# Reordering VectorE's splits and the index products of an extra block in a two-layer mixture-of-experts trunk

## The chip, the cores and the metric

One core of one Trainium2 chip runs the kernel. The metric is the device time of one launch in microseconds, the median of several executions. The engines are TensorE (PE in the profile, its weight loads PEld), VectorE (DVE), ScalarE (ACT), GpSimd (POOL) and SyncE (SP, which only issues transfers).

## The reference

Two layers over 512 tokens of width 1024, in float32. Each layer normalises and modulates the tokens, runs two mixers side by side (a chunked matrix memory and attention over a sliding window), merges them, and adds the result to the stream. After that comes the part that matters here, a mixture of 16 experts:

```
t = h.reshape(b * s, d)                      # 512 x 1024
scores = sigmoid(t @ w_router)               # 512 x 16
...                                          # best group of 4, best 2 experts in it
gates = sum(one_hot(idx) * wts)              # two weights for each token
for e in range(16):
    act = silu(t @ w_gate[e]) * (t @ w_up[e])        # 1024 -> 512, twice
    y = y + gates[:, e:e+1] * (act @ w_down[e])      # 512 -> 1024
```

The kernel computes an expert only for the tokens that chose it. The result has to agree with this float32 computation.

## The kernel before

**Experts.** `moe` runs once in each layer. Each expert gets a block of 128 token rows; the five experts with the fewest tokens, at places 4, 6, 8, 10 and 12 of the order (`SMALL`), get 64. An expert's rows are gathered from DRAM by an indirect transfer (`gather`), transposed on TensorE into `XT` (`turn`), multiplied by the gate and up weights (`gateup`), activated, transposed again (`turn_act`), multiplied by the down weights (`down`), and scattered to the DRAM tensor `y2d`. Experts overlap: the loop at the end of `moe` emits, for each expert e, `gateup(e)` with `turn_act(e - 1)` in its middle, then `turn(e + 1)`, then `down(e - 1)`.

**Splits.** A float32 product of a large expert is made of three products in a faster format. Each weight piece of 128 x 1024 is split into a high part `wh`, copied by ScalarE (L1535, L1587), and a low part `wl`, subtracted by VectorE (L1536, L1588); `mm3` (L116 to L118) then makes the products high by high, high by low and low by high. The tags `wh` and `wl` have three buffers each, so at most three pieces are split ahead. Small experts multiply the raw weights directly (L1465 gate and up, L1487 down), so during their gate and up products the split buffers are not needed. The experts in `DN` (all odd places up to 13) split their down weights as well, in four pieces. `turn` of a large expert also splits `XT`, into `XTh` (ScalarE, L1506) and `XTl` (VectorE, L1507), each in two halves.

**Weights.** SyncE streams the weights in chunks of 1 MB through 14 buffers. `pair_of_chunks` takes the next two chunks in a fixed order and issues the loads that may follow; the chunk that comes 14 later reuses a buffer.

**The further block.** An expert with more than 128 tokens spills into an extra block ("over"). `order_places` lists such blocks. `over_rows` reads the first of them: `overflow_next` (L2018 to L2022) writes its expert and block number, two registers are loaded from there (for SyncE and VectorE), and `pick` works out which tokens belong to it. `pick` is also used for the last expert (15), whose rows are combined by a product rather than by a scatter. It has three parts: VectorE builds a 0/1 matrix `osel` (L1634) and the right-hand sides `orv` (seven short operations, L1636 to L1641); TensorE makes eight products `oslot` of them (L1644); VectorE turns `oslot` into token numbers and weights with six short operations (L1645 to L1651; the further block has a seventh, L1665). Both picks share the tiles `osel`, `orv`, `own`, `osf` and `osl`, so VectorE can't fill `osel` for the further block until the products of the last expert's pick have read it. The results are used in `tail`, which has one branch without a further block and one with it.

**Order.** All of an engine's instructions run in one order, fixed when the kernel is built: a planner takes what its own estimates say is ready, earlier code first. Two tools override it. `tc.issue_after(x)` queues what is traced in its block on x's engine behind x; `queue(a, b)` queues b behind a. Neither makes an instruction wait for data. In the loop, `pick` for expert 15 stands after the body of expert 11, VectorE's part behind the activation product of expert 1, and `over_rows` after the body of expert 12, VectorE's part behind that of expert 2.

Of the kernel before, what the change touches and what calls it, by code (L numbers as in the profile page):

```python
# [41 lines left out]
NE = 16  # L42
# [13 lines left out]
DN = (1, 3, 5, 7, 9, 11, 13)  # L56
# [23 lines left out]
def tile_trunk(ctx, tc, x, c, w_ada, b_ada, w_norm1, w_in, conv_w, conv_b, b_igate, b_fgate, w_mnorm,  # L80
# [1252 lines left out]
    def moe(l, raw2, rt):  # L1333
# [110 lines left out]
        stt = {}  # L1444

        def turn_small(e):
# [4 lines left out]
            A.copy(XT, p)  # L1451
            stt["XT", e] = XT.rearrange("p (a b) -> p a b", a=8)

        def gateup_small(e, mid):

            XT = stt["XT", e]
            p = ps("gu")
            for half in range(2):
                if half and mid is not None:
                    mid()  # L1460
                chs = pair_of_chunks()
                for i in range(4):
                    kb = 4 * half + i
                    for g in range(2):
                        stt["gl"] = T.matmul(p[g * 64:g * 64 + 64], XT[:, kb], chs[g][:, i], start=kb == 0, stop=kb == KB - 1)  # L1465
            a_ = mp.tile([128, DE], F32, name="act")
            A.activation(a_[64:128], p[0:64], AF.Silu)
            stt["mul", e] = V.tensor_mul(a_[0:64], p[64:128], a_[64:128])
            stt["act", e] = a_
# [26 lines left out]
        def turn(e, XT=None):  # L1496
            if e in SMALL:
                return turn_small(e)
            if XT is None:
                XT = [mpx.tile([128, D], F32R, tag="XT", name=n, bufs=2).rearrange("p (a b) -> p a b", a=8) for n in ("XTh", "XTl")]  # L1500
            for q in range(2):
                p = ps("XT")
                for i in range(4):
                    T.transpose(p[:, i * 128:(i + 1) * 128], X[e % 2][:, (4 * q + i) * 128:(4 * q + i + 1) * 128], ident)  # L1504
                h_ = XT[0][:, 4 * q:4 * q + 4].rearrange("p a b -> p (a b)")
                A.copy(h_, p)  # L1506
                V.tensor_sub(XT[1][:, 4 * q:4 * q + 4].rearrange("p a b -> p (a b)"), p, h_)  # L1507
            stt["XT", e] = XT

        def turn_first(splits):  # L1510
# [66 lines left out]
        def down(e):  # L1577
            if e in SMALL:
                return down_small(e)
            aT = stt["aT", e]  # L1580
            wd = pair_of_chunks()
            Y = w4(e)
            pd = [ps("down0"), ps("down1")]
            for fb in range(4):
                if e in DN:
                    wh, wl = hl(2)
                    A.copy(wh.rearrange("p a b -> p (a b)"), wd[fb // 2][:, fb % 2])  # L1587
                    V.tensor_sub(wl.rearrange("p a b -> p (a b)"), wd[fb // 2][:, fb % 2], wh.rearrange("p a b -> p (a b)"))  # L1588
                for q in range(2):
                    if e in DN:  # L1590
                        mm3(pd[q], aT[:, 0, fb], aT[:, 1, fb], wh[:, q], wl[:, q], fb == 0, fb == 3)
                    else:
                        T.matmul(pd[q], aT[:, fb], wd[fb // 2][:, fb % 2, q * 512:(q + 1) * 512], start=fb == 0, stop=fb == 3)  # L1593
            for q in range(2):
                V.tensor_mul(Y[:, q * 512:(q + 1) * 512], pd[q], g2[:, q * 512:(q + 1) * 512])
            c = col(e)
            stt["put"] = G.indirect_dma_start(out=y2d, out_offset=bass.IndirectOffsetOnAxis(ap=slot[:, c:c + 1], axis=0),
                                              in_=Y, in_offset=None, bounds_check=2 * S - 1, oob_is_err=False)
# [29 lines left out]
        otok, ltok = [mp.tile([128, TB], F32, name=n, bufs=1) for n in ("otok", "ltok")]  # L1628
        ow, lw = [mp.tile([128, 1], F32, name=n, bufs=1) for n in ("ow", "lw")]

        def pick(e, places, tok, w):

            es_ = ds(e, 1) if not isinstance(e, int) else slice(e, e + 1)
            V.tensor_tensor(osel, places[:, :, None].to_broadcast([128, 2 * TB, 128]),  # L1634
                            iof[:, None, :].to_broadcast([128, 2 * TB, 128]), op=OP.is_equal)
            V.tensor_copy(orv[:, :, 0:2], rv.rearrange("p k t e c -> p (k t) e c")[:, :, es_, :].rearrange("p t o c -> p t (o c)"))  # L1636
            V.tensor_mul(own, top[:, :, :, es_].rearrange("p k t o -> p (k t o)"), wall.rearrange("p k t -> p (k t)"))
            for i in range(2, 5):
                V.tensor_copy(orv[:, :, i], own)
                if i < 4:  # L1640
                    V.tensor_sub(own, own, orv[:, :, i])  # L1641
            p = ps("oslot")
            for t in range(2 * TB):
                T.matmul(p[:, 0:5], osel[:, t], orv[:, t], start=t == 0, stop=t == 2 * TB - 1)  # L1644
            V.tensor_scalar(osf, p[:, 0:1], 4096.0, None, op0=OP.add)  # L1645
            V.tensor_add(osl[:, 0:1], p[:, 1:2], osf)
            V.tensor_reduce(w, p[:, 2:5], axis=AX.X, op=OP.add)

            V.tensor_single_scalar(osl[:, 1:2], osl[:, 0:1], 511 | 4096 | 8192, op=OP.bitwise_and)
            V.tensor_copy(osf, osl[:, 1:2])  # L1650
            V.tensor_sub(tok, osf.to_broadcast([128, TB]), firsts)  # L1651
# [6 lines left out]
        def over_rows():  # L1658

            overflow_next(posB)  # L1660
            e = nc.values_load(ovi[0:1, 0:1], engines=[ET.SP, ET.DVE], min_val=0, max_val=NE - 1)
            be = nc.values_load(ovi[0:1, 1:2], engines=[ET.DVE], min_val=0, max_val=2)
            V.tensor_copy(opos, posB[:, ds(be, 1), :].rearrange("p o t -> p (o t)"))
            pick(e, opos, otok, ow)
            V.tensor_single_scalar(ogi, osl[:, 0:1], 511, op=OP.bitwise_and)  # L1665
            return e

        def over_gather():
            G.indirect_dma_start(out=X[0], out_offset=None, in_=h2d[l],
# [229 lines left out]
        for e in range(NE):  # L1899
# [15 lines left out]
                down(e)  # L1915
            if e == NE - 5:
                with tc.issue_after(stt["mul", 1].ins):
                    pick(NE - 1, pk.rearrange("p k t -> p (k t)"), ltok, lw)
            if e == NE - 4:
                with tc.issue_after(stt["mul", 2].ins):  # L1920
                    oe = over_rows()
            if e == 1:
                with tc.issue_after(stt["mul", e].ins):
                    order_places()
# [21 lines left out]
        with none.Else():  # L1946
            with tc.If(n0 == 1) as one:
                tail(True)
            with one.Else():
                V.tensor_scalar(ovl, ovl, 1.0, None, op0=OP.add)  # L1950
                with tc.For_i(0, n0, 1):
                    e = over_rows()
                    over_gather()
                    turn(NE, XO)
                    oh, hl_ = over_block([over_chunk(e, i, raw2[0]) for i in range(6)])
                    for t in range(TB):
                        for i in range(2):
                            p = ps("rows")
                            for j in range(2):
                                T.matmul(p, oh[:, t * 128:(t + 1) * 128], hl_[j][:, i], start=j == 0, stop=j == 1)  # L1960
                            V.tensor_add(xt[t, i], xt[t, i], p)
                tail(False)
# [178 lines left out]
```

## Time and profile before

| what | value |
|---|---|
| median of 3 runs | 1427.54 us (1427.28 to 1436.03) |
| the profiled execution, its own time | 1431.1 us |
| its span, first to last instruction | 1429.2 us |
| mean granted TensorE clock | 0.974 |
| busy: PE, DVE, ACT, POOL | 93%, 70%, 47%, 14% |
| bytes moved by DMA | 365.09 MB, mean 255 GB/s |

The page's slices give busy tenths for each fortieth of the span (35.7 us). The experts of the first layer lie at about 428 to 716 us, those of the second at about 1100 to 1429 us. In this execution the first layer ends in the branch without a further block and the second in the branch with one. Times of the rows count from the first instruction; "idle before" names the engine's idle time ahead of an instruction and what ended it.

### The profile page before, as it was taken

To read this page: it belongs to the slowest core of one execution; us is meant where nothing else is said; L and a number is where in the kernel's file an instruction comes from. 1 tells how busy PE (TensorE), PEld (TensorE's weight loads), DVE (VectorE), ACT (ScalarE), POOL (GpSimd) and SP (SyncE) were. 2 spreads that over 40 slices of the span, in tenths; PEclk is the share of its full clock that TensorE was granted. 3 is DMA by queue.
4 is the path that set the end of the run, shared out by engine and by line. 5 is a ranking of instruction groups with operands and counts; after the bars stand their busy time and mean duration, and the time that the engine had idled before them with its cause. 6 is when DMAs were issued, how large, how long until landed. Compare 5 with 4: busy or idle time off the path is not lost.

```text
span 1429.2 us, 18477 instructions
## 1 busy us (share of the span) xinstructions
PE 1336.1 (93%) x6407; PEld 980.0 (69%) x6407; DVE 1005.8 (70%) x1941; ACT 678.4 (47%) x1184; POOL 206.4 (14%) x254
## 2 busy tenths in 40 slices
PE   2999999999989999979989999999998999997994
PEld 2776777778876666647568777777887766664662
DVE  5687756778578756657767666656858866765857
ACT  4254335444236545536356335444424655553652
POOL 7500020010011111210230000001001111211023
PEclk9998999999999999999999999999999999998998
DMA  9565465575868999999744433456566999999891
GB/s 313 204 222 164 131 247 177 182 234 181 301 223 278 361 380 381 378 369 384 263 158 148 147 108 129 155 200 170 200 249 238 314 350 390 378 376 381 324 365 64
DMA packets 166499, 365.09 MB, mean 255 GB/s; under 512 B 10549, under 2 KB 41517, under 8 KB 166136
## 3 DMA queue, kind: packets, MB, share of 16 engines
q1 hardware_dynamic: 152928, 327.71, 65.0%
q0 software_dynamic: 12752, 33.92, 6.9%
q10 hardware_dynamic: 712, 2.14, 0.5%
q8 instruction: 54, 0.88, 0.3%
q14 instruction: 53, 0.43, 0.1%
HBM read 346.27 MB, written 26.78 MB: 261 GB/s over the span
## 4 chain that ended last, share of the span: by engine, by line
PE 78%; DVE 11%; DMA 6%; ACT 2%; issue 2%; another core or an unknown queue 0%; ACTq 0%; POOL 0%; DVEq 0%; SPq 0%; POOLq 0%
PE winT L116 5%; PE winT L117 5%; PE winT L118 5%; PE gu L1465 5%; PE down L1593 3%; PE gate L117 3%; PE gate L116 3%; PE gate L118 3%; PE up L117 3%; PE up L118 3%; PE up L116 3%; DMA raw<-in_w_ada_dram 2%; PE downs L1487 2%; PE out L116 2%; PE out L118 2%; PE out L117 2%
## 5 line engine op out<-in xcount | busy, mean ns | idle before, releaser
L1535 ACT CAST wh<-raw 128x1024 fp32r<-128x1024 f32 x168 | 175.9, 1051 | 117.6 <-PE gate L118 82.3
L1536 DVE TENSOR_TENSOR wl<-raw,wh 128x1024 fp32r<-128x1024 f32 x168 | 201.8, 1221 | 34.1 <-ACT wh L1535 33.2
L116 PE MATMUL winT<-hh,wh 128*128 128x512 f32 x416 | 168.1, 405 | 0.5 <-DVE P L882 0.5
L117 PE MATMUL winT<-hl,wh 128*128 128x512 f32 x416 | 165.5, 398 | 0.0
L118 PE MATMUL winT<-hh,wl 128*128 128x512 f32 x416 | 165.3, 397 | 0.0
L483 ACT CAST wh<-raw 128x1024 fp32r<-128x1024 f32 (+1 forms) x59 | 54.2, 930 | 141.6 <-PE winT L117 86.3
L278 DVE SCALAR_TENSOR_TENSOR acc<-raw,cs,acc 128x1024 f32<-128x1024 f32 x70 | 89.6, 1280 | 32.7 <-DMA raw<-in_w_ada_dram 32.0
L116 PEld LDWEIGHTS winT<-hh,wh 128*128 128x128 f32 x416 | 78.9, 190 | 25.1 <-issue 5.1
L118 PEld LDWEIGHTS winT<-hh,wl 128*128 128x128 f32 x416 | 79.1, 190 | 18.7
L117 PEld LDWEIGHTS winT<-hl,wh 128*128 128x128 f32 x416 | 79.2, 190 | 17.6 <-DVE hl L463 0.3
L484 DVE TENSOR_TENSOR wl<-raw,wh 128x1024 fp32r<-128x1024 f32 (+1 forms) x57 | 60.3, 1067 | 25.6 <-ACT wh L483 25.5
L116 PE MATMUL gate<-wh,XTh 128*128 128x512 f32 x176 | 74.6, 424 | 3.0 <-ACT XTh L1523 2.6
L1465 PE MATMUL gu<-raw,XT 128*64 128x512 f32 x320 | 74.7, 597 | 0.7 <-DMA raw<-in_w_up_e_dram 0.7
L1588 DVE TENSOR_TENSOR wl<-raw,wh 128x1024 fp32r<-128x1024 f32 x56 | 66.5, 1219 | 12.0 <-ACT wh L1587 12.0
L117 PE MATMUL gate<-wl,XTh 128*128 128x512 f32 x176 | 73.1, 415 | 1.2 <-DVE wl L1536 1.2
L1395 POOL DMA_INDIRECT X<-h2d,gidx x30 | 38.5, 1283 | 238.7 <-PE XT L1504 103.1
L116 PE MATMUL up<-wh,XTh 128*128 128x512 f32 x176 | 69.9, 397 | 3.0 <-ACT wh L1535 3.0
L118 PE MATMUL gate<-wh,XTl 128*128 128x512 f32 x176 | 71.7, 407 | 0.5
L117 PE MATMUL up<-wl,XTh 128*128 128x512 f32 x176 | 70.2, 399 | 1.9 <-DVE wl L1536 1.9
L118 PE MATMUL up<-wh,XTl 128*128 128x512 f32 x176 | 69.6, 395 | 0.0
L1587 ACT CAST wh<-raw 128x1024 fp32r<-128x1024 f32 x56 | 57.0, 1048 | 13.9 <-PE down L118 7.9
L329 POOL DMA_DIRECT2D modd<-adarow x8 | 4.2, 531 | 406.4 <-DVE adarow L328 406.4
(530 smaller groups left out, 3044.0 us busy)
## 6 DMA issues: line engine op xcount, KB each, us to landing
raw<-in_w_down_e_dram SPq DMA_DIRECT2D x64, 1024.0 KB, 14.1
raw<-in_w_gate_e_dram SPq DMA_DIRECT2D x62, 1024.0 KB, 14.6
raw<-in_w_up_e_dram SPq DMA_DIRECT2D x62, 1024.0 KB, 14.7
raw<-in_w_ada_dram SPq DMA_DIRECT2D x40, 1024.0 KB, 5.1
raw<-in_w_in_dram SPq DMA_DIRECT2D x30, 1024.0 KB, 5.4
sch<-in_w_ada_dram SPq DMA_DIRECT2D x32, 256.0 KB, 6.5
raw<-in_w_out_dram SPq DMA_DIRECT2D x8, 1024.0 KB, 6.6
yk<-y2d SPq DMA_DIRECT2D x8, 1024.0 KB, 15.8
```

Of the source, the lines that this page charges most:

```text
L116: T.matmul(o, lh, rh, start=start, stop=False)
L117: T.matmul(o, lh, rl, start=False, stop=False)
L118: return T.matmul(o, ll, rh, start=False, stop=stop)
L278: V.scalar_tensor_tensor(self.acc, ch[:, a], cs[:, kb:kb + 1], self.acc, op0=OP.mult, op1=OP.add)
L483: A.copy(wh[:, :, a:b], src)
L484: (G if "first" in st else V).tensor_sub(wl[:, :, a:b], src, wh[:, :, a:b])
L1465: stt["gl"] = T.matmul(p[g * 64:g * 64 + 64], XT[:, kb], chs[g][:, i], start=kb == 0, stop=kb == KB - 1)
L1535: A.copy(wh, src)
L1536: stt["split"] = E.tensor_sub(wl, src, wh)
L1587: A.copy(wh.rearrange("p a b -> p (a b)"), wd[fb // 2][:, fb % 2])
L1588: V.tensor_sub(wl.rearrange("p a b -> p (a b)"), wd[fb // 2][:, fb % 2], wh.rearrange("p a b -> p (a b)"))
L1593: T.matmul(pd[q], aT[:, fb], wd[fb // 2][:, fb % 2, q * 512:(q + 1) * 512], start=fb == 0, stop=fb == 3)
```

## The change

There are two parts. `split_down` is a new function that makes one split of a down piece. In `gateup_small(e)`, behind the gate and up products and ahead of the activation, the two down chunks of expert e - 1 are taken from the stream and the first two of its four pieces are split; `down(e - 1)` then makes only the other two. In `turn(e + 1)` the first of the two subtractions of `XTl` is queued behind the second of these splits on VectorE. The two chunks keep their place in the stream, since nothing else takes a chunk between the old place and the new.

`pick` is cut in two: `pick` keeps VectorE's preparation, and `picked` has the eight products and what reads them. The last expert's `picked` moves from the body of expert 11 to that of expert 12, and `over_rows` follows it, no longer behind expert 2's activation product. The further block's `over_picked` moves to expert 14 and its products are queued behind the last gate and up product of that expert.

```
@@ -1451,6 +1451,13 @@
             A.copy(XT, p)
             stt["XT", e] = XT.rearrange("p (a b) -> p a b", a=8)
 
+        def split_down(e, fb):
+            wh, wl = hl(2)
+            src = stt["wd", e][fb // 2][:, fb % 2]
+            A.copy(wh.rearrange("p a b -> p (a b)"), src)
+            stt["sv"] = V.tensor_sub(wl.rearrange("p a b -> p (a b)"), src, wh.rearrange("p a b -> p (a b)"))
+            return wh, wl
+
         def gateup_small(e, mid):
 
             XT = stt["XT", e]
@@ -1463,6 +1470,10 @@
                     kb = 4 * half + i
                     for g in range(2):
                         stt["gl"] = T.matmul(p[g * 64:g * 64 + 64], XT[:, kb], chs[g][:, i], start=kb == 0, stop=kb == KB - 1)
+            if e - 1 in DN:
+                stt["wd", e - 1] = pair_of_chunks()
+                stt["sd", e - 1] = [split_down(e - 1, fb) for fb in range(2)]
+                stt["early"] = stt["sv"]
             a_ = mp.tile([128, DE], F32, name="act")
             A.activation(a_[64:128], p[0:64], AF.Silu)
             stt["mul", e] = V.tensor_mul(a_[0:64], p[64:128], a_[64:128])
@@ -1504,7 +1515,9 @@
                     T.transpose(p[:, i * 128:(i + 1) * 128], X[e % 2][:, (4 * q + i) * 128:(4 * q + i + 1) * 128], ident)
                 h_ = XT[0][:, 4 * q:4 * q + 4].rearrange("p a b -> p (a b)")
                 A.copy(h_, p)
-                V.tensor_sub(XT[1][:, 4 * q:4 * q + 4].rearrange("p a b -> p (a b)"), p, h_)
+                o = V.tensor_sub(XT[1][:, 4 * q:4 * q + 4].rearrange("p a b -> p (a b)"), p, h_)
+                if "early" in stt:
+                    queue(stt.pop("early"), o)
             stt["XT", e] = XT
 
         def turn_first(splits):
@@ -1578,14 +1591,13 @@
             if e in SMALL:
                 return down_small(e)
             aT = stt["aT", e]
-            wd = pair_of_chunks()
+            wd = stt["wd", e] = stt.get(("wd", e)) or pair_of_chunks()
             Y = w4(e)
             pd = [ps("down0"), ps("down1")]
+            sd = stt.get(("sd", e), [])
             for fb in range(4):
                 if e in DN:
-                    wh, wl = hl(2)
-                    A.copy(wh.rearrange("p a b -> p (a b)"), wd[fb // 2][:, fb % 2])
-                    V.tensor_sub(wl.rearrange("p a b -> p (a b)"), wd[fb // 2][:, fb % 2], wh.rearrange("p a b -> p (a b)"))
+                    wh, wl = sd.pop(0) if sd else split_down(e, fb)
                 for q in range(2):
                     if e in DN:
                         mm3(pd[q], aT[:, 0, fb], aT[:, 1, fb], wh[:, q], wl[:, q], fb == 0, fb == 3)
@@ -1628,7 +1640,7 @@
         otok, ltok = [mp.tile([128, TB], F32, name=n, bufs=1) for n in ("otok", "ltok")]
         ow, lw = [mp.tile([128, 1], F32, name=n, bufs=1) for n in ("ow", "lw")]
 
-        def pick(e, places, tok, w):
+        def pick(e, places):
 
             es_ = ds(e, 1) if not isinstance(e, int) else slice(e, e + 1)
             V.tensor_tensor(osel, places[:, :, None].to_broadcast([128, 2 * TB, 128]),
@@ -1639,6 +1651,9 @@
                 V.tensor_copy(orv[:, :, i], own)
                 if i < 4:
                     V.tensor_sub(own, own, orv[:, :, i])
+
+        def picked(tok, w):
+
             p = ps("oslot")
             for t in range(2 * TB):
                 T.matmul(p[:, 0:5], osel[:, t], orv[:, t], start=t == 0, stop=t == 2 * TB - 1)
@@ -1661,9 +1676,12 @@
             e = nc.values_load(ovi[0:1, 0:1], engines=[ET.SP, ET.DVE], min_val=0, max_val=NE - 1)
             be = nc.values_load(ovi[0:1, 1:2], engines=[ET.DVE], min_val=0, max_val=2)
             V.tensor_copy(opos, posB[:, ds(be, 1), :].rearrange("p o t -> p (o t)"))
-            pick(e, opos, otok, ow)
+            pick(e, opos)
+            return e
+
+        def over_picked():
+            picked(otok, ow)
             V.tensor_single_scalar(ogi, osl[:, 0:1], 511, op=OP.bitwise_and)
-            return e
 
         def over_gather():
             G.indirect_dma_start(out=X[0], out_offset=None, in_=h2d[l],
@@ -1915,10 +1933,13 @@
                 down(e)
             if e == NE - 5:
                 with tc.issue_after(stt["mul", 1].ins):
-                    pick(NE - 1, pk.rearrange("p k t -> p (k t)"), ltok, lw)
+                    pick(NE - 1, pk.rearrange("p k t -> p (k t)"))
             if e == NE - 4:
-                with tc.issue_after(stt["mul", 2].ins):
-                    oe = over_rows()
+                picked(ltok, lw)
+                oe = over_rows()
+            if e == NE - 2:
+                with tc.issue_after(stt["gl"].ins):
+                    over_picked()
             if e == 1:
                 with tc.issue_after(stt["mul", e].ins):
                     order_places()
@@ -1950,6 +1971,7 @@
                 V.tensor_scalar(ovl, ovl, 1.0, None, op0=OP.add)
                 with tc.For_i(0, n0, 1):
                     e = over_rows()
+                    over_picked()
                     over_gather()
                     turn(NE, XO)
                     oh, hl_ = over_block([over_chunk(e, i, raw2[0]) for i in range(6)])
```

## Rows read from the trace of the kernel before

**Rows 1.** The page: busy times, and the chain that ended last by engine.

```profile
PE 1336.1 (93%) x6407; PEld 980.0 (69%) x6407; DVE 1005.8 (70%) x1941; ACT 678.4 (47%) x1184; POOL 206.4 (14%) x254
...
PE 78%; DVE 11%; DMA 6%; ACT 2%; issue 2%; another core or an unknown queue 0%; ACTq 0%; POOL 0%; DVEq 0%; SPq 0%; POOLq 0%
```

**Rows 2.** Waits of TensorE over the whole span: in all, times, longest, in us.

```profile
PE oslot L1644 <- DVE orv L1639: 10.6, 2, 5.3
...
PE down L116 <- ACT wh L1587: 3.5, 2, 1.7
...
PE down L117 <- DVE wl L1588: 1.8, 2, 0.9
...
PE down L1593 <- ACT aT L1574: 3.0, 2, 1.5
```

**Rows 3.** Timeline of TensorE, first layer: start, duration, instruction, count, idle before.

```profile
629.77 0.73 PE L116 MATMUL down<-wh,aT 128*128 128x512 f32 x2 [1.75 <-ACT wh L1587]
...
637.94 0.39 PE L118 MATMUL down<-wh,aT 128*128 128x512 f32 x1
...
643.62 0.35 PE L1644 MATMUL oslot<-orv,osel 128*128 128x5 bf16 x8 [5.30 <-DVE orv L1639]
...
648.93 0.40 PE L116 MATMUL up<-wh,XTh 128*128 128x512 f32 x1
...
651.82 0.46 PE L1475 MATMUL aT<-ident,act 64*128 64x64 f32 x4
```

**Rows 4.** Stretches of the first layer: length, busy PE, PEld, DVE, ACT, POOL, PEclk, DMA, GB/s.

```profile
643.60:648.70 5.10, 5.08 (x20) 4.01 (x20) 1.69 (x8) 1.04 (x1) 0.00 (x0) 0.50 1.04 394
...
617.00:638.00 21.00, 17.64 (x78) 9.35 (x76) 10.85 (x18) 8.29 (x10) 2.98 (x2) 0.92 1.02 372
...
638.00:662.00 24.00, 18.70 (x86) 13.12 (x84) 17.48 (x30) 11.10 (x14) 1.92 (x2) 0.86 1.04 401
...
662.00:690.00 28.00, 26.49 (x110) 18.44 (x107) 20.07 (x23) 14.92 (x17) 2.95 (x3) 1.00 0.76 280
```

**Rows 5.** Timeline of VectorE, first layer, experts 10 to 13.

```profile
592.98 3.50 DVE L1588 TENSOR_TENSOR wl<-raw,wh 128x1024 fp32r<-128x1024 f32 x3 [0.25 <-ACT wh L1587]
...
619.00 1.22 DVE L1634 TENSOR_TENSOR osel<-opos,iof 128x1024 bf16<-128x1024 f32 x1
...
628.13 0.69 DVE L1507 TENSOR_TENSOR XTl<-XT,XTh 128x512 fp32r<-128x512 f32 x1 [6.79 <-PE gu L1465]
...
630.15 3.49 DVE L1588 TENSOR_TENSOR wl<-raw,wh 128x1024 fp32r<-128x1024 f32 x3
...
638.29 1.22 DVE L1536 TENSOR_TENSOR wl<-raw,wh 128x1024 fp32r<-128x1024 f32 x1
...
640.02 2.35 DVE L1536 TENSOR_TENSOR wl<-raw,wh 128x1024 fp32r<-128x1024 f32 x2
...
642.29 0.17 DVE L1636 COPY orv<-rv 128x16 bf16 x1
...
643.39 0.18 DVE L1639 CAST orv<-own 128x8 bf16<-128x8 f32 x1
```

**Rows 6.** Timeline of ScalarE, first layer, experts 12 and 15.

```profile
628.67 1.99 ACT L1587 CAST wh<-raw 128x1024 fp32r<-128x1024 f32 x2
...
631.31 1.05 ACT L1587 CAST wh<-raw 128x1024 fp32r<-128x1024 f32 x1 [0.64 <-DMA raw<-in_w_down_e_dram]
...
681.17 1.05 ACT L1535 CAST wh<-raw 128x1024 fp32r<-128x1024 f32 x1 [0.30 <-PE down L118]
```

**Rows 7.** Timeline of SyncE: two weight loads of the first layer are issued.

```profile
612.14 3.55 SPq L1381 DMA_DIRECT2D raw<-in_w_down_e_dram  x2
...
654.36 1.25 SPq L1381 DMA_DIRECT2D raw<-in_w_gate_e_dram  x1
```

**Rows 8.** DMA issues, one in each: the loads of rows 7, us from issue to landing.

```profile
raw<-in_w_down_e_dram SPq DMA_DIRECT2D x1, 1024.0 KB, 16.1
...
raw<-in_w_gate_e_dram SPq DMA_DIRECT2D x1, 1024.0 KB, 18.3
```

More of the change, by code (lines that the diff above doesn't have):

```diff
@@ L1452, in turn_small, with split_down @@
             stt["XT", e] = XT.rearrange("p (a b) -> p a b", a=8)
+        def split_down(e, fb):
+            wh, wl = hl(2)
+            src = stt["wd", e][fb // 2][:, fb % 2]
+            A.copy(wh.rearrange("p a b -> p (a b)"), src)
+            stt["sv"] = V.tensor_sub(wl.rearrange("p a b -> p (a b)"), src, wh.rearrange("p a b -> p (a b)"))
+            return wh, wl
         def gateup_small(e, mid):
@@ L1465, in gateup_small @@
                         stt["gl"] = T.matmul(p[g * 64:g * 64 + 64], XT[:, kb], chs[g][:, i], start=kb == 0, stop=kb == KB - 1)
+            if e - 1 in DN:
+                stt["wd", e - 1] = pair_of_chunks()
+                stt["sd", e - 1] = [split_down(e - 1, fb) for fb in range(2)]
+                stt["early"] = stt["sv"]
             a_ = mp.tile([128, DE], F32, name="act")
@@ L1506, in turn @@
                 A.copy(h_, p)
-                V.tensor_sub(XT[1][:, 4 * q:4 * q + 4].rearrange("p a b -> p (a b)"), p, h_)
+                o = V.tensor_sub(XT[1][:, 4 * q:4 * q + 4].rearrange("p a b -> p (a b)"), p, h_)
+                if "early" in stt:
+                    queue(stt.pop("early"), o)
             stt["XT", e] = XT
@@ L1580, in down @@
             aT = stt["aT", e]
-            wd = pair_of_chunks()
+            wd = stt["wd", e] = stt.get(("wd", e)) or pair_of_chunks()
             Y = w4(e)
             pd = [ps("down0"), ps("down1")]
+            sd = stt.get(("sd", e), [])
             for fb in range(4):
                 if e in DN:
-                    wh, wl = hl(2)
-                    A.copy(wh.rearrange("p a b -> p (a b)"), wd[fb // 2][:, fb % 2])
-                    V.tensor_sub(wl.rearrange("p a b -> p (a b)"), wd[fb // 2][:, fb % 2], wh.rearrange("p a b -> p (a b)"))
+                    wh, wl = sd.pop(0) if sd else split_down(e, fb)
                 for q in range(2):
@@ L1629, in moe, with pick @@
         ow, lw = [mp.tile([128, 1], F32, name=n, bufs=1) for n in ("ow", "lw")]
-        def pick(e, places, tok, w):
+        def pick(e, places):
             es_ = ds(e, 1) if not isinstance(e, int) else slice(e, e + 1)
@@ L1641, in pick, with picked @@
                     V.tensor_sub(own, own, orv[:, :, i])
+        def picked(tok, w):
             p = ps("oslot")
@@ L1663, in over_rows, with over_picked @@
             V.tensor_copy(opos, posB[:, ds(be, 1), :].rearrange("p o t -> p (o t)"))
-            pick(e, opos, otok, ow)
+            pick(e, opos)
+            return e
+        def over_picked():
+            picked(otok, ow)
             V.tensor_single_scalar(ogi, osl[:, 0:1], 511, op=OP.bitwise_and)
-            return e
         def over_gather():
@@ L1917, in moe @@
                 with tc.issue_after(stt["mul", 1].ins):
-                    pick(NE - 1, pk.rearrange("p k t -> p (k t)"), ltok, lw)
+                    pick(NE - 1, pk.rearrange("p k t -> p (k t)"))
             if e == NE - 4:
-                with tc.issue_after(stt["mul", 2].ins):
-                    oe = over_rows()
+                picked(ltok, lw)
+                oe = over_rows()
+            if e == NE - 2:
+                with tc.issue_after(stt["gl"].ins):
+                    over_picked()
             if e == 1:
@@ L1952, in moe @@
                     e = over_rows()
+                    over_picked()
                     over_gather()
```

## Prediction

> **What bounds the kernel now.** I read the page first: TensorE is busy 93% of the span and carries 78% of the chain that ended last [rows 1]. So only time in which TensorE stands still, or runs slowly, can be won. Next I listed what TensorE waits for. Its longest wait is the one the change points at: `oslot` on `orv`, twice, 5.3 us each, once in each layer. Beside it stand two short waits of the down products on their splits, 1.7 and 0.9 us in each layer, and one of 1.5 us on `aT` [rows 2].
>
> The timeline shows the place. `down` of expert 11 can start at 629.77, after 1.75 us of idling, and ends at about 638.2 (its last product starts at 637.94 and takes 0.23 of TensorE's time). The next instruction is the first `oslot` of the further block, at 643.62. Twelve gate products follow up to 648.93, in 5.1 us, 0.43 each; the next twelve, up to the transposes at 651.82, take 2.9, some 0.23 each, TensorE's usual pace [rows 3]. There the first half of expert 13 ends. The granted clock over 643.6 to 648.7 is 0.50, the lower of its two levels (1.2 GHz), after the engine had stood still; it is below 1 as well, 0.92 on average, over 617 to 638, where the two short waits lie [rows 4]. VectorE shows why `orv` is late: in its order it stands behind three splits of expert 13, and starts at 642.29 [rows 5].
>
> The second thing to see is the weight stream. The DMA engines are at 1.02 to 1.04 of their time from 617 to 662, at 372 to 401 GB/s, and fall to 0.76 only after that [rows 4]. A faster TensorE meets weights that come no sooner.
>
> **The change part by part.** *(a) The further block's products leave the place behind `down` of expert 11.* Removed there: 5.3 us of standing still, and the low clock after it, 12 products at 0.43 instead of 0.23, 2.3 us. The eight products are moved, not removed. What is late next: the splits of expert 13. VectorE's first `wl` ends at 639.5, the next two at 641.2 and 642.4 [rows 5]. A piece feeds six products, 1.4 us. So without the stop the first piece is done at 639.5 + 5 x 0.23 = 640.7, the second at 642.4, the third at 643.9. The fourth needs a buffer that the first frees (cast 1.05, subtraction 1.22, ready at 643.6), and is done at 645.4. Before, the same four pieces ended at 651.8. Gain: 6.4 us.
>
> Against that stands VectorE's own work for the picks. The last expert's products now come after the body of expert 12, so what depends on them may fall behind `down` of 11 too: six short operations like the one at 643.39 (1.0 us), `osel` (1.22 us, at 619.00 before), `orv` (642.29 to 643.57, 1.3 us) [rows 5]. Pieces go round a ring of three buffers: cast 1.05, subtraction 1.22, products 1.4 and about 0.5 for two hand-overs (the first is 0.3 in [rows 6]) make 4.2 us, and TensorE uses three pieces in 4.2. So VectorE time put into that ring is lost. With all 3.5 us in it the gain is 2.9 us, with none 6.4. I take `orv` where it is now, behind the third split, and the rest beside the transposes and small down products: 5.1 us.
>
> TensorE itself waits for nothing new at the last expert's products: their `orv` is filled long before, their results are wanted in `tail`. The further block's stand behind expert 14's gate and up products, over 20 us after `orv`; 0.4 us of TensorE each, as before. SyncE reads the block's expert number from what VectorE writes; that read stands among the weight loads as before, and a late one would hold them. With 16 to 18 us from issue to landing [rows 8] some 6 MB are on the way, so a hold below 10 us starves nothing. GpSimd gets nothing new.
>
> *(b) Two down splits first on VectorE.* At experts 4, 6, 8 and 10 they already are: at expert 10 three splits run in one piece from 592.98, ahead of activation and `XTl` [rows 5]. Only at expert 12 does VectorE stand at an `XTl` for 6.79 us, until the gate and up products free its buffer at 628.13, with the splits behind it [rows 5]. Only there can the change matter. The stop of 1.75 us is ScalarE's cast, which starts at 628.67 [rows 6]. Its chunk was issued at 612.14 and took 16.1 us: it landed at 628.2, just as the gate and up products ended at 628.0 [rows 3, 7, 8]. So the cast can come 0.4 us earlier at most. VectorE's first `wl` starts at 630.15 although the cast ends at 629.7: another 0.4. But the activation product and both `XTl`, 2.0 us, which ran during the wait for the cast, then fall between the second and the third split. The third piece's chunk, cast at 631.31 after a wait for DMA, sets that split: it ends at about 635.0 instead of 633.6 (630.15 + 3.49). Bounds: 0.5 us lost, 1.0 won; I take 0.3 won, since both ends hang on one late chunk.
>
> Taking the two chunks earlier changes no order among SyncE's loads, and the stream is full.
>
> *Sum.* 5.1 + 0.3 = 5.4 us in each layer. The second layer has the same waits [rows 2], so 10.8 us for both. **The cap.** Expert 15's chunks are the test. Its first lands at 654.36 + 18.3 = 672.7, the next some 2.7 us later (1 MB at 386 GB/s, between 372 and 401), at 675.4. ScalarE casts the third piece from it at 681.17, 5.8 us later, and ahead of the `aT` that TensorE waits for [rows 2, 6 to 8]. So nearly all of 5.4 us fits, and not much more. DMA has (1 - 0.76) x 28 = 6.7 us of room in 662 to 690 [rows 4], so the tail's loads can follow.
>
> How the weights go is where a page bears. The Trainium skill, "HBM Reference", section Specifications (TRN2), gives a core that streams alone about 425 GB/s. Here the full stretches show 372 to 401. By the page's figure a chunk would take an estimated 2.5 us, the stream would gain on TensorE, and the cap would not bind; the sum would then be its upper bound, 14.8 us.
>
> The profiled execution took 1431.1 us, 3.6 above the median. For it the sum gives 1420.3; for the median 1427.5 - 10.8 = **1416.7**.
>
> **The rivals.** *VectorE takes the place of the wait.* All its picking work lies in the ring: 2.9 us a layer, less 0.5: 2.4, so 1422.7. For it: the new code puts the last expert's products behind `down` of 11. Against: in the rows of before, that work filled idle time. Chance 0.22.
>
> *The weights don't bind so early, and nothing of the picking is in the way:* 6.4 + 1.0 = 7.4 a layer, 14.8 in all: 1412.7; with the low clock around the short waits gone too (21 x (1 - 0.92) = 1.7 us a layer [rows 4]) 1409.3. For: the DMA share falls after 662. Against: the cap. Chance 0.14.
>
> *The stream is the bound already:* the time comes back as waits for `raw`, 1 us a layer is left, 1425.5. For: the DMA share of 1.04. Against: the third piece of expert 15 has its chunk 5.8 us before its cast. Chance 0.07. The Trainium skill, "DMA: Bandwidth & Descriptors", section Where 436 GB/s comes from, says that for transfers from HBM the memory side binds at about 358 GB/s; by it the stretch would be bound all through, and the sum some 2 us. The trace is above that figure, at 372 to 401, and does not agree.
>
> *Slower: the clock.* The long stop goes, but short waits for `wl` stay at the start of expert 13. If the clock, low behind 629.7, stays low through its 48 products, that is 48 x 0.2 = 9.6 us, and with some 1.5 us of waits 11.1 against the 5.3 + 2.3 removed: 3.5 us lost a layer, 1434.5. It decides if the granted clock is still 0.5 at 649 us; with expert 14 low as well, another 9.6 a layer, it is 1453.7. Against: after each stop here it was back in about 5 us of unbroken products [rows 3, 4]. Chance 0.05.
>
> *The change does not do what it says:* the old place is filled by the last expert's products. They have their operands, so nothing is lost; this is in the forecast.
>
> **The numbers.** Forecast 0.52, spread over 4.3 to 6.4 us a layer: 1414.7 to 1418.9. The range of 8 in 10 takes in the first rival, and the second down to 1410: 1410 to 1424.5. A measurement of this kernel can't tell less than about 1% from no change, here 14.3 us, 1413.3. Faster by more than that needs the second rival and a little of the forecast: 0.16. Slower by over 1%: the last rival whole, since a clock that stays low would hardly stop at one expert: 0.05. Within 1%: 0.79.
>
> **What would show it.** In the changed trace: no wait of `oslot` on `orv`; eight `oslot` products behind the gate and up products of expert 14; VectorE's order at expert 12 with two L1588 ahead of L1507; the first half of expert 13 ending 5 to 6 us sooner after expert 12's products; a clock of 1.00 there; `aT` of expert 14 no longer waiting, or waiting on a cast that waits for DMA (the cap). I am wrong if TensorE's idle time at experts 12 and 13 shrinks and the time up to the last scatter does not, or if `osel` and `orv` stand between the splits of expert 13 and hold them by over 3 us.

## The result and the profile after

| | median, us | runs | ratio to the kernel before, 95% interval |
|---|---|---|---|
| before | 1429.55 (1423.71 to 1436.03) | 8 | |
| after | 1420.89 (1416.95 to 1425.86) | 8 | 0.9938 (0.9914 to 0.9962) |

The change saves 0.6%, some 8.9 us (5.4 to 12.3). The profiled execution took 1419.82 us, its span is 1418.0.

What TensorE waits for, whole span (us in total, times, longest):

```profile
PE gate L117 <- DVE wl L1549: 5.8, 6, 2.3
PE down L117 <- DVE wl L1458: 5.4, 8, 1.2
PE down L116 <- ACT wh L1457: 3.6, 2, 1.8
```

and one line of the kernel before that belongs beside them:

```profile
PE gate L117 <- DVE wl L1536: 1.2, 4, 0.4
```

The wait of `oslot` on `orv` [rows 2] is gone. The waits on `wl` have grown, on the gate products from 1.2 to 5.8 us, on the down products from 1.8 [rows 2] to 5.4. TensorE's timeline in the first layer shows where they are (start, duration, in brackets the idle time ahead and its releaser):

```profile
629.05 0.73 PE L116 MATMUL down<-wh,aT 128*128 128x512 f32 x2 [1.83 <-ACT wh L1457]
629.63 0.35 PE L1659 MATMUL oslot<-orv,osel 128*128 128x5 bf16 x8
...
634.50 0.50 PE L117 MATMUL down<-wl,aT 128*128 128x512 f32 x1 [1.18 <-DVE wl L1458]
...
636.89 0.40 PE L116 MATMUL gate<-wh,XTh 128*128 128x512 f32 x1
...
649.73 3.65 PE L1498 MATMUL downs<-raw,aT 128*64 128x512 f32 x16
...
656.13 0.50 PE L117 MATMUL gate<-wl,XTh 128*128 128x512 f32 x1 [2.32 <-DVE wl L1549]
```

Expert 15's index products stand inside `down` of expert 11. Expert 13's gate follows that `down` at 636.89 without a gap, 7 us earlier than before [rows 3]. Then, at expert 14, TensorE stands still for 2.32 us. VectorE shows why:

```profile
628.05 0.69 DVE L1479 TENSOR_TENSOR act<-gu,act 64x512 f32<-64x512 f32 x1
629.03 2.36 DVE L1458 TENSOR_TENSOR wl<-raw,wh 128x1024 fp32r<-128x1024 f32 x2 [0.28 <-ACT wh L1457]
631.42 0.69 DVE L1518 TENSOR_TENSOR XTl<-XT,XTh 128x512 fp32r<-128x512 f32 x1
...
632.10 1.22 DVE L1646 TENSOR_TENSOR osel<-opos,iof 128x1024 bf16<-128x1024 f32 x1
633.23 2.35 DVE L1458 TENSOR_TENSOR wl<-raw,wh 128x1024 fp32r<-128x1024 f32 x2
...
653.43 1.39 DVE L1502 TENSOR_TENSOR Y<-downs,g 64x512 f32<-64x512 f32 x2 [1.97 <-PE downs L1498]
654.85 3.50 DVE L1549 TENSOR_TENSOR wl<-raw,wh 128x1024 fp32r<-128x1024 f32 x3
```

Two down splits do stand early at expert 12. `osel` then stands ahead of the third, which makes the 1.18 us above. And the `Y` of expert 12, which needs TensorE's down products, stands ahead of expert 14's first splits, although ScalarE had cast the high parts of the first two by 652.67, 2.2 us before VectorE takes them up:

```profile
650.68 1.99 ACT L1548 CAST wh<-raw 128x1024 fp32r<-128x1024 f32 x2 [0.25 <-DMA raw<-in_w_gate_e_dram]
```

In the kernel before, the two stood the other way round:

```profile
656.89 2.36 DVE L1536 TENSOR_TENSOR wl<-raw,wh 128x1024 fp32r<-128x1024 f32 x2 [0.66 <-ACT wh L1535]
...
662.60 1.39 DVE L1491 TENSOR_TENSOR Y<-downs,g 64x512 f32<-64x512 f32 x2 [0.42 <-PE downs L1487]
```

The granted clock in four stretches of after (length, busy time and pieces of PE, PEld, DVE, ACT, POOL, then clock, DMA share, GB/s): expert 13; the end of the stop at expert 14 in the first layer; what follows it there; what follows the same stop in the second layer.

```profile
637.00:649.70 12.70, 12.70 (x61) 9.88 (x59) 9.74 (x12) 7.61 (x9) 1.80 (x1) 1.00 1.03 396
653.30:656.10 2.80, 0.51 (x3) 0.19 (x1) 2.62 (x4) 1.04 (x1) 1.00 (x1) 1.00 1.04 402
656.10:662.00 5.90, 5.87 (x27) 4.83 (x28) 4.93 (x5) 3.39 (x4) 0.76 (x1) 1.00 1.02 406
1321.30:1327.00 5.70, 5.70 (x20) 4.63 (x21) 3.52 (x4) 1.75 (x3) 0.73 (x1) 0.72 1.03 413
```

Expert 13 runs at full clock, where its first half had 0.50 [rows 4]. Behind the stop at expert 14 the clock stays full in the first layer and is 0.72 in the second.

**One measure for all kernels.** In both profiles, and in those of the experiments, time is counted from the end of expert 10's last down product. Given is how long after it expert 12's down products start, expert 14's up products end, and expert 15's last product ends.

| kernel | layer 1, us | layer 2, us | ratio to before |
|---|---|---|---|
| before | 41.6, 57.0, 93.1 | 40.9, 56.4, 92.9 | |
| before, again | 41.3, 56.8, 92.8 | 40.9, 56.4, 92.8 | 0.9985 (0.9958 to 1.0011) |
| after | 32.2, 51.1, 87.0 | 31.7, 52.1, 88.5 | 0.9938 (0.9914 to 0.9962) |
| after, again | 32.7, 51.6, 87.5 | 31.8, 52.0, 88.4 | 0.9959 (0.9938 to 0.9981) |
| picks only | 31.7, 52.2, 88.1 | 32.4, 51.3, 87.6 | 0.9957 (0.9931 to 0.9982) |
| splits only | 38.6, 54.1, 90.2 | 38.6, 54.1, 90.5 | 0.9998 (0.9973 to 1.0023) |
| order at 14 | 32.0, 48.4, 84.3 | 31.8, 48.1, 84.4 | 0.9893 (0.9856 to 0.9930) |
| order at 14, again | 32.1, 48.4, 84.4 | 31.7, 48.1, 84.4 | 0.9904 (0.9868 to 0.9941) |
| `orv` early | 35.4, 55.7, 91.1 | 34.2, 54.7, 90.5 | 0.9987 (0.9961 to 1.0013) |
| `orv` early, order at 14 | 34.7, 51.0, 86.4 | 34.2, 50.6, 86.4 | 0.9931 (0.9908 to 0.9955) |
| `osel` later | 35.5, 51.9, 87.8 | 35.0, 51.4, 87.7 | 0.9954 (0.9933 to 0.9975) |
| cast first | 32.7, 49.1, 85.0 | 33.6, 49.9, 86.3 | 0.9922 (0.9898 to 0.9945) |
| all early | 30.9, 47.7, 83.3 | 32.1, 48.5, 84.6 | 0.9907 (0.9875 to 0.9938) |
| all early, old place | 31.4, 47.7, 83.1 | 32.1, 48.5, 84.3 | 0.9902 (0.9867 to 0.9937) |

So after gains 9.4 and 9.2 us up to expert 12, gives 3.5 and 4.9 back by the end of expert 14, and keeps 6.1 and 4.4.

### The profile page after: what moved, and what is told of

The parts are those of the page before. It is cut to its first block, busy times and chain, and to the rows that moved or that the text cites. A ratio compares the mean times of both kernels' runs of the same rounds, so it can differ in the third digit from the quotient of the medians.

```text
span 1418.0 us, 18485 instructions
## 1 busy us (share of the span) xinstructions
PE 1328.5 (94%) x6407; PEld 973.3 (69%) x6407; DVE 1005.3 (71%) x1941; ACT 679.1 (48%) x1184; POOL 207.1 (15%) x254
## 4 chain that ended last, share of the span: by engine, by line
PE 43%; DVE 5%; issue 1%; DMA 1%; ACT 1%; another core or an unknown queue 0%; POOL 0%; DVEq 0%; ACTq 0%; SPq 0%; POOLq 0%
PE winT L116 4%; PE winT L117 3%; PE winT L118 3%; PE gu L1472 3%; PE gate L117 2%; PE down L1605 1%; PE up L117 1%; PE gate L118 1%; PE up L118 1%; PE gate L116 1%; PE up L116 1%; PE downs L1498 1%; PE tok L118 1%; PE tok L116 1%; PE out L116 1%; PE out L118 1%
## 5 line engine op out<-in xcount | busy, mean ns | idle before, releaser
L1458 DVE TENSOR_TENSOR wl<-raw,wh 128x1024 fp32r<-128x1024 f32 x56 | 66.8, 1220 | 10.8 <-ACT wh L1457 10.8
```

The costliest lines, as they stand in the source:

```text
L1458: stt["sv"] = V.tensor_sub(wl.rearrange("p a b -> p (a b)"), src, wh.rearrange("p a b -> p (a b)"))
```

## The experiments

**One part alone.** Picks only: the changed kernel without

```
-            if e - 1 in DN:
-                stt["wd", e - 1] = pair_of_chunks()
-                stt["sd", e - 1] = [split_down(e - 1, fb) for fb in range(2)]
-                stt["early"] = stt["sv"]
```

> The changed kernel without its early down splits: only the picking is parted and moved. My theory (the wait of the first index product on orv is the whole change, 5 us a layer and more behind it; the early splits are worth 0.3 us a layer): 0.993 to 0.996 of the kernel before, within 2 us of the changed kernel's 8.9 us gain, no wait oslot<-orv, the product of expert 14's first gate half still waiting some 2 us for wl. The rival (the early splits carry a good part, since VectorE has room only before the last half of XT's rest): half the gain, 0.997 or more, with waits on wl at expert 12 of 2 us and more in each layer.

Splits only: the changed kernel with the picking where it was.

```
                     pick(NE - 1, pk.rearrange("p k t -> p (k t)"))
+                    picked(ltok, lw)
             if e == NE - 4:
-                picked(ltok, lw)
-                oe = over_rows()
-            if e == NE - 2:
-                with tc.issue_after(stt["gl"].ins):
+                with tc.issue_after(stt["mul", 2].ins):
+                    oe = over_rows()
                     over_picked()
```

> The changed kernel with the further block's picking back in its old place: only the early splits are left. My theory: within 0.2% of the kernel before (0.998 to 1.001), the wait oslot<-orv still at 10 us in two pieces, a wait of down(11) on wh of under 2 us a layer. The rival (the splits carry a part of their own): 0.997 or less.

Picks only keeps 5.0 and 5.3 us a layer, as much as the whole change: my theory. Its ratio, 0.9957, lies in the range that I gave. Splits only met its forecast in time (0.9998, and the wait on `orv` stays), but not the theory behind it: the stretch is 2.9 and 2.4 us shorter, where 0.3 was expected. TensorE's timeline of splits only:

```profile
628.13 0.50 PE L117 MATMUL down<-wl,aT 128*128 128x512 f32 x1 [0.53 <-DVE wl L1458]
628.47 0.40 PE L118 MATMUL down<-wh,aT 128*128 128x512 f32 x1
...
639.21 0.35 PE L1659 MATMUL oslot<-orv,osel 128*128 128x5 bf16 x8 [5.53 <-DVE orv L1651]
```

and of the kernel before at the same product:

```profile
631.42 0.62 PE L117 MATMUL down<-wl,aT 128*128 128x512 f32 x1 [0.92 <-DVE wl L1588]
631.84 0.63 PE L118 MATMUL down<-wh,aT 128*128 128x512 f32 x1
```

The wait of 0.92 us became 0.53, and the products behind it run at full pace instead of half. The clock over all of `down` of 11 is 0.80 before and 1.00 here:

```profile
629.80:638.20 8.40, 7.48 (x24) 5.49 (x25) 5.58 (x6) 5.06 (x5) 0.00 (x0) 0.80 1.01 366
```

```profile
626.90:633.60 6.70, 6.17 (x24) 4.32 (x25) 5.61 (x6) 5.06 (x5) 0.00 (x0) 1.00 1.05 382
```

The timed runs of splits only show none of these 5 us; that is taken up below.

**VectorE's order at expert 14.** The changed kernel, and where `gateup(14)` splits its gate chunk:

```
+                        if e == NE - 2 and half == 0 and p is pg and j == 1:
+                            queue(stt["split"], stt["Y", e - 2])
```

`stt["Y", 12]` is expert 12's first `Y` product.

> The changed kernel, and on VectorE expert 14's first two gate splits stand ahead of expert 12's two Y products. Theory (what was given back at expert 14 is VectorE's order alone: two splits whose ScalarE half is long done stand behind a Y that waits for the down products): the wait of expert 14's first gate product falls from 2.3 us to under 0.5 in both layers, the low clock behind it in the second layer goes, and the time is 3 to 8 us under the changed kernel's, 0.988 to 0.992 of the kernel before. Rival (the stream of weights is the next limit): the wait moves to the ScalarE casts and their DMA one or two chunks later, and the time stays within 1.5 us of the changed kernel's, 0.993 to 0.995.

> The changed kernel with expert 14's first two gate splits ahead of expert 12's Y products, once more: 0.987 to 0.992 of the kernel before, the stretch from expert 10's last product to expert 15's last 84.3 us in both layers, if what it gave the first time was the order and not the run.

```profile
652.31 2.36 DVE L1550 TENSOR_TENSOR wl<-raw,wh 128x1024 fp32r<-128x1024 f32 x2
654.59 1.38 DVE L1502 TENSOR_TENSOR Y<-downs,g 64x512 f32<-64x512 f32 x2
```

```profile
654.30:657.10 2.80, 2.80 (x12) 2.28 (x13) 2.75 (x4) 1.63 (x2) 0.85 (x1) 1.00 1.04 391
1323.90:1329.60 5.70, 5.70 (x31) 4.75 (x30) 5.37 (x7) 3.87 (x5) 1.76 (x1) 1.00 1.03 410
```

VectorE's order and two windows of the first of the two runs: TensorE is busy all through where it had stood, and the clock is full. What after gave back is kept, 8.8 and 8.5 us a layer, and 8.7 and 8.5 in the second run. It was VectorE's order, and not the stream, which ran at 391 to 410 GB/s meanwhile.

**The wait without the move.** The kernel before; only the register load is parted, so that the planner is free to place VectorE's early:

```
-            e = nc.values_load(ovi[0:1, 0:1], engines=[ET.SP, ET.DVE], ...)
+            e, ev = [nc.values_load(ovi[0:1, 0:1], engines=[g], ...) for g in (ET.SP, ET.DVE)]
...
-            pick(e, opos, otok, ow)
+            pick(ev, opos, otok, ow)
```

> The kernel before, in which only the register load of the further block's expert is parted: SyncE and VectorE each load the number by themselves, so that VectorE's copies into orv come to stand behind osel, in its idle time at expert 12, and the index products stay at expert 12 without their wait. Theory (the wait was the cost, not the place of the products): the wait oslot<-orv is gone and the time is that of picks only within 2 us, 0.993 to 0.996 of the kernel before. Rival (the place counts: the 5 us were cover for weights that come no earlier, or the VectorE work at expert 12 costs as much): 0.997 or more.

```profile
620.67 1.22 DVE L1634 TENSOR_TENSOR osel<-opos,iof 128x1024 bf16<-128x1024 f32 x1
622.73 0.17 DVE L1636 COPY orv<-rv 128x16 bf16 x1
```

```profile
632.67 0.36 PE L1644 MATMUL oslot<-orv,osel 128*128 128x5 bf16 x8
...
660.83 0.79 PE L117 MATMUL gate<-wl,XTh 128*128 128x512 f32 x1 [2.32 <-DVE wl L1536]
```

`orv` stands in VectorE's idle time, the wait is gone, and still hardly anything was gained. I had said 0.993 to 0.996, so as a forecast this missed, and the time, 0.9987, is the rival's. But the loss is the known one: at expert 14 the same 2.32 us, again behind `Y`, with the low clock behind it (0.72 over 658 to 664). With the order at expert 14 on top:

> The kernel of the parted register load (index products at expert 12, without their wait) with, on VectorE, expert 14's first two gate splits ahead of expert 12's two Y products. In its trace the parted load alone had brought expert 12's down products 6.1 and 6.7 us earlier after expert 10's, and 4.8 and 5 us of that were lost up to the end of expert 14's gate and up. Theory (place does not count, VectorE's order at expert 14 took the gain back): nothing is lost there, the stretch from expert 10's last product to expert 15's last goes from 91 to 86 or 87 us in each layer, 0.989 to 0.993 of the kernel before. Rival (products at expert 12 hold up the weights' splits for good): the stretch stays at 90 us or more, 0.997 or more.

The stretch falls to 86.4 us in both layers, the ratio to 0.9931, at the edge of what I had said. So what expert 14 took back was VectorE's order here too. Some 2 us a layer remain against the order at expert 14, and the two kernels differ in the early splits as well as in the place, so this run alone does not say that the place costs nothing. A part of it is a wait of 1.00 us on `wl` at expert 13's first gate product, where `Y` of expert 11 stands ahead of the split. The place by itself is tried below.

**What else stands ahead of a split.** On top of the order at expert 14, `osel` is queued behind the last down split of 11, and both halves of `XTl` behind the early ones (the changed kernel queues one half, and the planner puts the other first):

```
-                    queue(stt.pop("early"), o)
+                    queue(stt["early"], o)
...
+            if behind:
+                queue(behind, sel)
```

> The kernel with expert 14's splits ahead, and besides on VectorE the further block's osel behind expert 11's last down split, and both halves of XTl behind the two early splits. Theory (each thing that stands on VectorE ahead of a split that TensorE waits for costs its own time): the waits of down(11) on wl fall from 0.3 and 1.1 us to under 0.3, the stretch from expert 10's last product to expert 15's last falls by 0.5 to 1.5 us from 84.3 us, the time by 1 to 3 us, 0.987 to 0.991 of the kernel before. Rival (the chunk's landing, shown by the cast's own wait of 0.9 us on its DMA, sets the third split anyway): no change against 84.3 us.

```profile
637.17 1.22 DVE L1650 TENSOR_TENSOR osel<-opos,iof 128x1024 bf16<-128x1024 f32 x1
639.00 1.29 DVE L1611 TENSOR_TENSOR Y<-down,g 128x512 f32<-128x512 f32 x2 [0.62 <-PE down L118]
```

```profile
641.75 0.50 PE L117 MATMUL gate<-wl,XTh 128*128 128x512 f32 x1 [2.10 <-DVE wl L1551]
```

A miss, and 3.4 us a layer lost. `osel` left the third down split, but it and expert 11's two `Y` then stood ahead of expert 13's first split, and TensorE waited 2.10 us there. There was also less to win than I had thought: the 1.1 us that I meant lies at expert 13's down products. With the order at expert 14 the third split of 11 made TensorE wait in neither layer, since `down` of 11 ran at a low clock there (0.79 over 629.9 to 638.0).

On top of that, ScalarE's first two down casts ahead of the Silu of expert 12:

```
+            if e == NE - 4:
+                queue(stt["sc"], silu)
```

> The kernel before this one in the list, and on ScalarE expert 11's first two down casts ahead of expert 12's Silu. Theory (the chunk has landed, and ScalarE's order alone makes the 1.75 us wait of the first down product on wh): that wait falls to under 0.5 us in both layers, the stretch is another 1 to 1.5 us shorter than its 83.5 us, 0.985 to 0.990 of the kernel before. Rival (the stream of weights binds here: the chunk lands only about when expert 12's gate and up end): the cast waits for its DMA instead, and the stretch stays as it is or grows by the Silu's 0.6 us.

```profile
630.44 1.99 ACT L1457 CAST wh<-raw 128x1024 fp32r<-128x1024 f32 x2 [6.40 <-DMA raw<-in_w_down_e_dram]
632.46 0.59 ACT L1478 ACTIVATE act<-gu 64x512 f32<-64x512 f32 x1
```

The first wait fell from 2.04 us only to 1.22 in the first layer, where the cast waits for its DMA, and from 1.75 to 0.30 in the second. The ratio, 0.9922, misses the range I gave. The rival holds for the first layer: there the stream does set the cast. It is a gain on `osel` later, not on the order at expert 14 alone, and new waits of 1.28 us on `wl` and 0.90 on `wh` follow in the first layer.

**All of it together.** The order at expert 14, the same order at expert 13 (first gate split ahead of both `Y` of 11), the parted load, and the last expert's products in their old place:

```
+                        if e in (NE - 3, NE - 2) and half == 0 and p is pg and j == e - NE + 3:
+                            for y_ in stt["Y", e - 2]:
+                                queue(stt["split"], y_)
```

> The changed kernel with four things set by VectorE's order: the parted register load and the last expert's products at their old, early place (so that osel and orv of both stand in VectorE's idle time ahead of expert 12's Silu product), the first gate split of expert 13 ahead of expert 11's two Y products, and two of expert 14's ahead of expert 12's. Theory (nothing but what stands on VectorE ahead of a split that TensorE waits for is left): down(11)'s third split no longer makes TensorE wait (1.1 us before), expert 13's gate does not wait as it did with osel behind the splits (2.1 us), the stretch from expert 10's last product to expert 15's last is 82.5 to 84 us in both layers, the time 0.985 to 0.990 of the kernel before. Rival (the weights' landing sets the third split and what follows): 84.3 us or more, as with expert 14's order alone.

The same with the further block's products back at expert 12:

> The same kernel with the further block's products back at expert 12, where they find orv ready: place alone. Theory (place does not count once nothing waits): within 0.7 us a layer of the kernel before it in the list. Rival (at expert 12 the products and the short operations behind them cost TensorE and the splits their own time, and the place behind expert 14 hides it): 1 to 2 us a layer more.

TensorE in `down` of 11 with all early, first and second layer, and the clock over it in each:

```profile
628.09 0.50 PE L117 MATMUL down<-wl,aT 128*128 128x512 f32 x1 [0.53 <-DVE wl L1458]
1295.75 0.80 PE L117 MATMUL down<-wl,aT 128*128 128x512 f32 x1 [0.53 <-DVE wl L1458]
```

```profile
626.80:633.70 6.90, 6.34 (x25) 4.64 (x26) 6.86 (x7) 5.13 (x6) 0.00 (x0) 1.00 1.02 370
1294.00:1303.00 9.00, 7.99 (x27) 6.18 (x28) 7.74 (x9) 6.00 (x7) 0.00 (x0) 0.81 1.04 380
```

In this stretch no wait over 0.9 us is left in either but the first cast's 1.75. The forecast for all early, 82.5 to 84 us and 0.985 to 0.990, held in the first layer only (83.3, but 84.6 in the second, and 0.9907). The first layer is 1 us shorter than with the order at expert 14, the second is not: there `down` of 11 still runs at a clock of 0.81 behind a wait of 0.53 us. The first layer also shows what `osel` had cost in after: at the same full clock, with `osel` early, the third split makes no wait, and `down` of 11 ends 18.3 instead of 19.5 us after expert 10's. Place alone makes 0.2 and 0.3 us: the theory. In time, these two and the two runs of the order at expert 14 can't be told apart (0.9893 to 0.9907).

**Two kernels again.**

> The kernel before, unchanged, against itself: how far two sets of runs of one kernel lie apart, and which stretches of its profile vary from run to run. 0.997 to 1.003; from expert 10's last product to expert 15's last 92.5 to 93.5 us in both layers, as in its first profile, while the stretch between the two layers' experts (384 us in the first profile) may differ by 3 us.

> The changed kernel once more, beside the others: 0.991 to 0.996 of the kernel before, and in its profile 87 to 88.5 us from expert 10's last product to expert 15's last, with the wait of expert 14's first gate half on wl of 2.3 us in both layers, as in its first profile.

Both as expected; the stretch repeats within 0.5 us. From expert 15's last product to the second layer's first gate it is 383.7 us in both profiles of before, 382.6 and 382.8 in those of after, and 387.6 and 386.6 in those of the order at expert 14, though the edits touch nothing there.

## Why the prediction was right

The range held the time, and the sum, 10.8 us, is near the stretch's 10.5 (6.1 + 4.4) but above the timed 8.9 and, again, 5.9 us. The 1420.9 us lies above the forecast's own 1414.7 to 1418.9; 2 us of that is the base, 1427.5 from three runs against 1429.55 from eight. Time alone does not tell the forecast from the first rival, which had 4.8 us; the traces do. And that the sum came out was partly luck. Step by step:

- **(a)** 5.1 us a layer forecast; picks only gives 5.0 and 5.3. But it got there by two errors that cancel, and that is the luck. I had priced 7.6 us removed at most and 6.4 left after the splits of expert 13. Up to expert 12's down products 9.9 and 8.5 us came. The first layer has more because `down` of 11 began 1.4 us sooner after expert 10's, 0.69 of it a wait for a chunk that this profile of before has and this one has not, and then took 7.7 instead of 8.6 us, at a clock of 1.00 instead of 0.80; in the second layer it took 8.6 as before. The clock ahead of the stop I had counted in the second rival only. In after, the first half of expert 13 ended 7.5 us sooner after expert 12's gate and up products, where I had said 5 to 6. And the bound was not where I put it, in the ring at expert 13, but at expert 14, where some 5.0 and 3.5 us went back.
- **The order that flipped.** This is what the prediction did not see. By the profiles, `Y` of expert 12 stands ahead of expert 14's first splits in both layers of after, picks only and `orv` early, where the wait of `oslot` is gone, and behind them in before and splits only, where it stays. The planner fixes VectorE's order by its own estimates; that it reckoned `down` of 12 earlier is the likely reason, but no run shows its estimates. The Trainium skill, "PSUM — Partial Sum Buffer", section Engine vs sequencer instructions, has VectorE's queue as strict first in, first out. The trace agrees: two ready splits wait behind a `Y` whose products end at 653.4.
- **The picking work.** I left 1.3 us of 3.5 in the ring. `osel` stood ahead of the third down split, not among expert 13's, and cost 1.18 us there. The first rival, "VectorE takes the place of the wait", was right in kind, with the wrong instruction and place.
- **(b)** 0.3 us a layer forecast. In the stretch, alone 2.9 and 2.4, on top of (a) 1.1 and -0.9. The mis-sized term is the clock in `down` of 11, which the forecast left out and only the second rival had priced, at 1.7 us: it took 8.6 us in both layers of the kernel before and 6.8 in both with splits only, where no half pace follows the shorter wait. In the first layer 0.69 us more is the wait for a chunk named under (a).
- **The cap** was wrong. The order at expert 14 keeps 8.8 us, well above 5.8, and the casts of expert 15 wait for no DMA there. The loads did come hardly sooner, as I had said: in its second run expert 15's first chunk was issued 36.3 us after expert 10's last product, where it had been 37.0, and landed at 54.5 instead of 55.3. But the cast of the third piece, my test, came only 5.6 us sooner (58.2 instead of 63.8), and TensorE's first product for expert 15, 63.6 us after expert 10's last where it had been 72.0, still lies 9 us behind the landing of its chunk. I had taken the time of a cast for the time at which TensorE needs the piece. The issue of that chunk, its time to landing, and the first product, in that run:

```profile
654.31 1.23 SPq L1381 DMA_DIRECT2D raw<-in_w_gate_e_dram  x1
...
raw<-in_w_gate_e_dram SPq DMA_DIRECT2D x1, 1024.0 KB, 18.2
...
681.60 0.48 PE L116 MATMUL gate<-wh,XTh 128*128 128x512 f32 x1
```

- **Second rival** (weights don't bind, 7.4 us a layer, 9.1 with the low clock gone): that is the state that the order at expert 14 reaches, with 8.8 and 8.5 us in the stretch. Its times, 1415.0 and 1418.2 us, stay above that rival's 1412.7; by the ratios it saves some 15 and 14 us, where the rival had 14.8.
- **The stream as the bound** fell: TensorE did not wait for it at experts 13 and 14. The Trainium skill, "HBM Reference", section Specifications (TRN2), has about 425 GB/s for a core that streams alone; the highest stretch here shows 413.
- **The clock as a loss** did not come as I priced it, but its place is real: in the second layer the stop at expert 14 took the clock to 0.72.

**Open.** In nearly every comparison the timed gain is 2 to 5 us less than the stretch's: for after 8.9 and 5.9 against 10.5, for splits only 0.3, at most 3.9, against 5.3. Two things on record bear on it.

A profile is one execution: the second one of after took 1419.98 us, the fastest of its twelve (median 1425.79), so its stretches need not be those of the median.

Outside the stretch, too, the granted clock shifts with the edits. Over the first 160 us behind expert 15, in pieces of 40, it is 0.91, 1.00, 0.91, 1.00 before and 0.96, 1.00, 0.91, 0.96 in the second run of the order at expert 14, but 0.96, 1.00, 0.96, 1.00 after. Over the first 20 us of the second layer's experts it is 1.00 before and after, and 0.83 in both profiles of the order at expert 14, which end expert 4's down products 2.2 us later after the first gate product (107.8 instead of 105.7). So in these two profiles 5 to 6 us are lost from expert 15 of the first layer to expert 10 of the second (585.6 and 584.6 us instead of 579.6); why the clock differs there is not known. In after nothing was lost there (578.6), so this does not explain its difference.

Nor can I say in time that the early splits alone are worth anything: `orv` early with the order at expert 14 and all early at the old place, which differ by the early splits and the order at expert 13, lie 3.3 and 2.1 us apart in the stretch, but their intervals overlap.

## What to carry to other kernels

On an engine that works in order, what stands ahead of a ready instruction counts, not how busy the engine is: after taking a wait away, look at which instruction there now waits for the engine that you have just sped up. When a planner fixes the order, one edit can flip a pair far behind it; pin the pairs that matter. And measure the profile in stretches between two events: here a stretch repeats within some 0.5 us in two profiles of one kernel, while single runs of one kernel lie up to 17 us apart.

## What was not expected of the hardware

The same stop had two outcomes in after: 2.32 us at expert 14 left the first product behind it at 0.50 us and the clock at 1.00 in the first layer, and 2.31 us was followed by 0.72 in the second. A wait of 0.53 us in all early was followed by full pace in the first layer and by half pace in the second, and one of 1.18 us (after) by full pace. From the length of a stop alone the clock behind it could not be told.
